# A causal convolution accumulated in the projection's PSUM bank, with buffer counts and stage order changed beside it

## The chip, the cores and the metric

The kernel runs on one core of a Trainium2 chip. The metric is the device time of one execution in microseconds. The engines are TensorE (PE, with its weight loads PEld), VectorE (DVE), ScalarE (ACT), GpSimd (POOL) and SyncE (SP, which here issues most DMAs). Each engine works through its own queue in order; semaphores tie the queues together.

## The reference

One layer of a decoder block over 2048 tokens of width 1024, in float32. Two mixers run side by side: four gated-DeltaNet heads and four retention heads, all of width 128. Then come the output projection, a gated MLP (5632 columns up, with a convolution of width 3) and a last norm. Cut to the part that matters here:

```python
n = _rms_norm(h, attn_norm_w[l])
proj = jnp.einsum('bsd,dc->bsc', n, w_in[l])
(gq, gk, gv, gg, ga, gb, rq, rk, rv, rg) = jnp.split(proj, split_idx, axis=-1)
# gated DeltaNet: short causal conv (4 taps) on q, k and v, then silu
qkv = jax.nn.silu(_causal_dwconv(jnp.concatenate([q, k, v], axis=-1), conv_w))
q = _l2norm(q) * (d ** -0.5); k = _l2norm(k)
# per chunk of 64: a triangular solve, and a recurrence over the chunks
t_mat = triangular_solve(eye + m, eye)
u = u_b - w_c @ state;  o = qd_c @ state + qk_c @ u
state = state * cd_c + kd_c.T @ u
# retention heads, concatenation, out projection, residual
h = h + jnp.einsum('bsm,md->bsd', mix, w_out[l])
n2 = _rms_norm(h, mlp_norm_w[l])
h = h + _conv_glu_mlp(n2, w_up[l], mlp_conv_w[l], w_down[l])
```

## The kernel before

A float32 product is made of three passes on TensorE: each operand is split into a high part and a rest, and `mm3` (lines 117 to 122) adds high x high, high x rest and rest x high in one PSUM bank. So nearly everything on PE comes in triples of rows, L120, L121 and L122, or L542 to L544 for the retention and gate projections.

The mixers work on four blocks b = 0 to 3 of 512 tokens. What is done for a block is cut into stages, and the string `ORDER` lists the stages of all blocks in the order in which the program is written out: "0a3" is stage a3 of block 0. The stages that matter here:

- aH: projection, convolution and Silu of k and q of DeltaNet head H (`proj_kq`); fH: the same for v (`proj_v`).
- cH: transposes of k and q (`kqtr`, L702), their norms, the products k kᵀ and k qᵀ (`kk`, L732), and the write of the matrix N to DRAM (`gdn_z`, L768). eH transposes v.
- bP: the inverse of 32x32 triangular blocks of head pair P on POOL (L784, L786), a round trip through DRAM (L789, L797) and a transpose on DVE (L799). lP: the two doubling levels, with `yps` (L814, L834) and `ttps` (L822, L841).
- rPc: step c of the recurrence of pair P: `ks` (L865), DVE L868, `wps` (L876), DVE L879, `sps` (L885), DVE L892 or L898.
- hH and yH: retention head H: `rtr` (L990), `rkk` (L996), the decay on DVE (L997), `ro` (L1011 and L1013), then L1016 on ACT and L1023 on DVE.
- dH the decay matrix, k, q, v the retention projections, p, P, g, G the gates, W and S the output projection as seven products of half matrices, O and Q the making of its weights (POOL L297, ACT L305, DVE L306), N the second norm, U a piece of the MLP's up projection.

`ORDER` sets the order of the program only. Below it a scheduler fixes the order of each engine's queue, and gives tiles their places: the numbers of buffers (`BUFS` for SBUF tiles, `NPB`, `NPM` and `NPR` for the three PSUM pools "bk", "mx" and "rc", which share the eight banks) are upper bounds that steer it. So a small edit may move instructions far from it.

A convolution of one head runs like this. PE makes the product `chm` in a bank of pool "bk": 24 matmuls of 128x512. DVE multiplies it by the row of inverse norms into the first half of an SBUF tile `ca` (L667, in `scaled`). ACT copies this, times the last tap, to the second half of `ca` (L414). DVE adds the other three taps there (L417), for b > 0 the three tokens of the block before (L421), and keeps the last three tokens for the next block (L423). ACT takes the Silu from the second half into the tile `ykq` (L680), or for v back into `ca` (L688). So the bank is free again after L667. A tile `ca` is two halves of 128x512, and the four heads of a block take twelve of them.

Of the kernel before, what the change touches and what calls it, by code (L numbers as in the profile page):

```python
# [10 lines left out]
AF = mybir.ActivationFunctionType  # L11
ALU = mybir.AluOpType
# [16 lines left out]
NWV = 5  # L29
FX = (0, 2, 4, 1, 5)  # L30
NU = 4
NPB = 9
NPM = 4
NPR = 10
NRAW = 3
NLATE = 4
NXR = 8
FD = 6
BUFS = {"n1": 8, "ykq": 3, "kv": 7, "NT": 7, "AT": 9, "o": 6, "n2s": 15, "xk": 2, "og": 1, "co": 6, "Cw": 3, 
        "wx": 1, "wsq": 5, "wvr": 1, "wvt": 8, "ca": 12, "mix": 5, "D": 6, "rk": 14, "rq": 4, "rv": 9,   # L40
        "sm": 6, "sc": 16, "wg": 2, "kt": 4, "Ar": 2, "Nb": 6, "rot": 1, "rrow": 6}

ORDER = ("0pro 0k0 0v0 0dec 0q0 0d0 0a0 0c0 0a1 0d1 0a2 0c1 0f1 0f0 0b0 0e0 0d2 0e1 0c2 0h0 0y0 0h1 0f2 "
# [11 lines left out]
P = 128  # L55
S = 2048
D = 1024
KT = D // P
TB = 512
NB = S // TB  # L60
NT = TB // P
# [10 lines left out]
U1 = 1024  # L72
# [147 lines left out]
def mixers(ctx, tc, base, base_used, marks, drp, mm3, gamma, mhalf, n1w, n2w, gcw, gv127, epsr, gnw, n2d, hd,  # L220
# [6 lines left out]
    PE, ACT, DVE, POOL = nc.tensor, nc.scalar, nc.vector, nc.gpsimd  # L227
# [4 lines left out]
    psm = ctx.enter_context(tc.tile_pool(name="psm", bufs=NPM, space=PSUM))  # L232
    psr = ctx.enter_context(tc.tile_pool(name="psr", bufs=NPR, space=PSUM))

# [40 lines left out]
    ghalo = pc(12, 3)  # L275
# [109 lines left out]
    def al(tag, shape, dt=F32):  # L385
        return unit(ap_, tag, shape, dt, **({"bufs": BUFS[tag]} if tag in BUFS else {}))

    def half(owner, key, tag, i):

        if key not in owner:  # L390
            owner[key] = al(tag, [P, 2, TB])
        return owner[key][:, i]
# [20 lines left out]
    def conv(ps, acc, wt, halo, first, ntap):  # L413
        ACT.activation(acc, ps, AF.Copy, scale=wt[:, ntap - 1:ntap])  # L414
        for s in range(1, ntap):
            w = wt[:, ntap - 1 - s:ntap - s]
            DVE.scalar_tensor_tensor(acc[:, s:], ps[:, :TB - s], w, acc[:, s:], op0=ALU.mult, op1=ALU.add)  # L417
        if not first:
            for s in range(1, ntap):
                w = wt[:, ntap - 1 - s:ntap - s]  # L420
                DVE.scalar_tensor_tensor(acc[:, :s], halo[:, ntap - 1 - s:], w, acc[:, :s],  # L421
                                         op0=ALU.mult, op1=ALU.add)
        DVE.tensor_copy(halo, ps[:, TB - (ntap - 1):])  # L423

    def A_items(b, st):
# [233 lines left out]
        def chmajor(w, i):  # L659
            n1 = st["n1"]  # L660
            ps = bank("chm")
            mm3(ps, [wcol(w, i, k) + (n1[k][:, 0], n1[k][:, 1]) for k in range(KT)])
            return ps

        def scaled(ps):
            ca = al("ca", [P, 2, TB])
            DVE.tensor_tensor(ca[:, 0], ps, st["rrow"], op=ALU.mult)  # L667
            return ca[:, 0], ca[:, 1]


        def proj_kq(h):
            def f(w):
                hd_ = st["hd", h] = {}
                ykq = hd_["ykq"] = al("ykq", (P, 2, TB))
                for i in range(2):
                    ps = chmajor(w, i)
                    ci = (4 if i == 0 else 0) + h
                    cin, acc = scaled(ps)
                    conv(cin, acc, gcw[:, ci], ghalo[:, ci], b == 0, 4)
                    ACT.activation(ykq[:, i], acc, AF.Silu)  # L680
            return f

        def proj_v(h):
            def f(w):
                ps = chmajor(w, 0)
                cin, acc = scaled(ps)
                conv(cin, acc, gcw[:, 8 + h], ghalo[:, 8 + h], b == 0, 4)
                ACT.activation(acc, acc, AF.Silu)  # L688
                st["hd", h]["v"] = acc
            return f  # L690

        def gdn_kq(h):
# [842 lines left out]
```

## Time and profile before

| | us |
|---|---|
| median of 3 runs (lowest to highest) | 2435.12 (2432.28 to 2436.66) |
| the profiled execution | 2431.43 |
| its span | 2429.6 |
| PE busy in it | 2382.8 (98%) |
| DVE busy | 1639.0 (67%) |
| ACT busy | 1052.5 (43%) |
| POOL busy | 448.7 (18%) |

The mixers fill about the first 1150 us of the span, the MLP's two projections the rest. A row of a group, as "L417 DVE ... x144 | 109.9, 763 | 20.0 <-ACT ca L414 19.0", has the line, engine, operation, output and inputs, the count, the busy time in us, the mean of one in ns, then the idle time of the engine just before them and what ended most of it. A row of a waits view has what waited for what, us in all, how often, and the longest. A row of a timeline has start and length in us, and in brackets the idle time before it and what ended it. A matmul of 128x512 is shown some 0.39 us long, but one starts every 0.227 us.

### The profile page before, as it was taken

Reading aid. Unit: us, or ns where it says so; the run is one execution under the profiler, and the core shown is the slowest. Engines: PE = TensorE matmul, PEld = TensorE weight load, DVE = VectorE, ACT = ScalarE, POOL = GpSimd, SP = SyncE. Lnnn points to the kernel's source line nnn. Section 1 sums busy time; section 2 is a strip of 40 time slices with the busy share of each in tenths; the row PEclk is TensorE's granted clock in tenths of the full one; section 3 lists DMA queues with packets and bytes.
Section 4 is the critical chain, followed back from the end, with each engine's and each line's share of the span. In section 5 each row is a group of like instructions: output and inputs, shape, how many; then the busy total and the mean of one; then the engine's idle time right before and its main releaser. Section 6 shows DMA issues by size and latency. Waiting matters only on the chain.

```text
span 2429.6 us, 35733 instructions
## 1 busy us (share of the span) xinstructions
PE 2382.8 (98%) x12364; PEld 1999.4 (82%) x12364; DVE 1639.0 (67%) x3137; ACT 1052.5 (43%) x2256; POOL 448.7 (18%) x745
## 2 busy tenths in 40 slices
PE   9998999999999999999999999999999999999998
PEld 8877888878887888887888888878888888888887
DVE  5866776664635673668988888995556676554773
ACT  6545555644444463356643434432222234332341
POOL 0166114520044003310101100100000002431020
PEclk9999999999999999999999999999999999999999
DMA  6877799895756865687977779877768588774782
GB/s 241 301 279 249 306 332 346 317 347 210 268 201 239 334 209 178 239 322 286 348 292 290 296 293 362 308 256 243 250 231 313 199 272 277 253 228 141 226 254 102
DMA packets 305414, 646.09 MB, mean 266 GB/s; under 512 B 50833, under 2 KB 130129, under 8 KB 305233
## 3 DMA queue, kind: packets, MB, share of 16 engines
q1 hardware_dynamic: 288512, 629.51, 72.7%
q10 hardware_dynamic: 16720, 14.30, 1.9%
q8 instruction: 97, 1.59, 0.3%
q14 instruction: 85, 0.69, 0.1%
HBM read 437.82 MB, written 205.88 MB: 265 GB/s over the span
## 4 chain that ended last, share of the span: by engine, by line
PE 51%; DVE 2%; issue 1%; ACT 0%; DMA 0%; POOLq 0%; POOL 0%; ACTq 0%
PE p L120 11%; PE p L121 11%; PE p L122 11%; PE d L122 6%; PE d L120 6%; PE d L121 6%; PE wo L122 0%; PE wo L120 0%; PE wo L121 0%; DVE x L1146 0%; DVE acc L1275 0%; DVE st L1167 0%; DVE uc L1228 0%; DMA wur<-in_w_u 0%; PE nps L1124 0%
## 5 line engine op out<-in xcount | busy, mean ns | idle before, releaser
L121 PE MATMUL p<-x,wu 128*128 128x512 f32 x1176 | 457.6, 389 | 0.0
L120 PE MATMUL p<-x,wu 128*128 128x512 f32 x1176 | 453.2, 390 | 1.1 <-ACT wu L1145 0.8
L122 PE MATMUL p<-x,wu 128*128 128x512 f32 x1176 | 451.1, 389 | 0.0
L120 PEld LDWEIGHTS p<-x,wu 128*128 128x128 f32 x1176 | 220.7, 188 | 49.1 <-DVE uc L1228 1.3
L121 PEld LDWEIGHTS p<-x,wu 128*128 128x128 f32 x1176 | 220.7, 188 | 45.9 <-DVE x L1146 0.5
L122 PEld LDWEIGHTS p<-x,wu 128*128 128x128 f32 x1176 | 220.7, 188 | 45.7
L1275 DVE SCALAR_TENSOR_TENSOR acc<-uc,base,acc 128x1022 f32<-128x1022 f32 (+1 forms) x176 | 220.7, 1278 | 38.0 <-ACT acc L1272 37.9
L1228 DVE TENSOR_TENSOR uc<-p,uc 128x512 f32<-128x512 f32 x224 | 153.0, 686 | 119.7 <-PE p L122 117.8
L542 PE MATMUL tok<-wc,n 128*128 128x512 f32 (+2 forms) x576 | 199.7, 353 | 7.2 <-ACT n L458 5.3
L543 PE MATMUL tok<-wc,n 128*128 128x512 f32 (+2 forms) x576 | 199.9, 349 | 0.0
L544 PE MATMUL tok<-wc,n 128*128 128x512 f32 (+2 forms) x576 | 195.4, 347 | 0.0
L191 POOL TENSOR_TENSOR vt<-vr 128x512 f32<-128x512 f32 x44 | 71.1, 1618 | 640.4 <-DMA vr<-in_w_d 464.0
L120 PE MATMUL d<-v,uu 128*128 128x512 f32 x448 | 174.3, 389 | 0.0
L121 PE MATMUL d<-v,uu 128*128 128x512 f32 x448 | 174.3, 389 | 0.0
L122 PE MATMUL d<-v,uu 128*128 128x512 f32 x448 | 174.3, 389 | 0.0
L120 PE MATMUL chm<-n,wc 128*128 128x512 f32 x384 | 152.2, 397 | 0.1
L122 PE MATMUL chm<-n,wc 128*128 128x512 f32 x384 | 151.2, 394 | 0.0
L121 PE MATMUL chm<-n,wc 128*128 128x512 f32 x384 | 151.0, 393 | 0.0
L1272 ACT ACTIVATE acc<-uc,base 128x1024 f32<-128x1024 f32 x88 | 97.1, 1144 | 80.7 <-DVE uc L1228 32.9
L542 PEld LDWEIGHTS tok<-wc,n 128*128 128x128 f32 x576 | 110.2, 192 | 20.2 <-ACT n L458 5.6
L417 DVE SCALAR_TENSOR_TENSOR ca<-ca,base 128x511 f32<-128x511 f32 (+1 forms) x144 | 109.9, 763 | 20.0 <-ACT ca L414 19.0
L543 PEld LDWEIGHTS tok<-wc,n 128*128 128x128 f32 x576 | 110.7, 192 | 12.5
(285 smaller groups left out, 5028.8 us busy)
## 6 DMA issues: line engine op xcount, KB each, us to landing
wu<-wu SPq DMA_DIRECT2D x308, 512.0 KB, 6.3
wc<-wd SPq DMA_DIRECT2D x116, 512.0 KB, 6.5
wv<-kW SPq DMA_DIRECT2D x112, 512.0 KB, 6.9
wc<-kP SPq DMA_DIRECT2D x84, 512.0 KB, 6.5
ur<-au SPq DMA_DIRECT2D x56, 512.0 KB, 5.7
wd<-wc SPq DMA_DIRECT2D x44, 512.0 KB, 4.7
wur<-in_w_u SPq DMA_DIRECT2D x44, 512.0 KB, 6.3
au<-st SPq DMA_DIRECT2D x88, 256.0 KB, 5.0
```

The lines of the kernel that those rows point to most:

```text
L120: PE.matmul(ps, ah, bh, start=(first and i == 0), stop=False, skip_group_check=chk)
L121: PE.matmul(ps, ah, bl, start=False, stop=False, skip_group_check=chk)
L122: PE.matmul(ps, al, bh, start=False, stop=(i == n - 1), skip_group_check=chk)
L191: POOL.tensor_tensor(tt[:, j], a, b_, op=ALU.subtract)
L417: DVE.scalar_tensor_tensor(acc[:, s:], ps[:, :TB - s], w, acc[:, s:], op0=ALU.mult, op1=ALU.add)
L542: PE.matmul(ps, ah, wh, start=(k == 0), stop=False)
L543: PE.matmul(ps, ah, wl, start=False, stop=False)
L544: PE.matmul(ps, al_, wh, start=False, stop=(k == KT - 1))
L1228: add = lambda o, ps, a: DVE.tensor_tensor(o, ps, a, op=ALU.add)
L1272: ACT.activation(acc, u, AF.Copy, scale=mcw[:, ci, 2:3])
L1275: DVE.scalar_tensor_tensor(acc[:, t:], u[:, :T2 - t], w, acc[:, t:], op0=ALU.mult, op1=ALU.add)
```

## The change

The change has three parts, and the diff has all of them.

First, `scaled` goes, and `conv_silu(ps, out, ci)` takes the place of three calls. The multiply by the row of inverse norms writes into the tile in which the result will stand: a half of `ykq` for k and q, a half of `ca` for v. The Copy with the last tap then writes into the product's own bank, the multiply-adds accumulate in that bank, and the Silu reads the bank and writes over the scaled input. `conv` itself is the same function with other arguments. For v, two heads share one `ca` tile, so that a block takes two of them.

Second, upper bounds of pools are changed: one more for "bk", one less for "rc", and fifteen counts of SBUF tiles.

Third, `ORDER` is another permutation of the stages. In the diff below its first line stands for it.

```diff
-NPB = 9
+NPB = 10
 NPM = 4
-NPR = 10
+NPR = 9
...
-BUFS = {"n1": 8, "ykq": 3, "kv": 7, "NT": 7, "AT": 9, "o": 6, "n2s": 15, "xk": 2, "og": 1, "co": 6, "Cw": 3, 
-        "wx": 1, "wsq": 5, "wvr": 1, "wvt": 8, "ca": 12, "mix": 5, "D": 6, "rk": 14, "rq": 4, "rv": 9, 
-        "sm": 6, "sc": 16, "wg": 2, "kt": 4, "Ar": 2, "Nb": 6, "rot": 1, "rrow": 6}
+BUFS = {"n1": 8, "ykq": 3, "kv": 9, "NT": 7, "AT": 9, "o": 8, "n2s": 17, "xk": 2, "og": 2, "co": 6, "Cw": 5, 
+        "wx": 1, "wsq": 5, "wvr": 1, "wvt": 7, "ca": 11, "mix": 3, "D": 7, "rk": 14, "rq": 4, "rv": 8, 
+        "sm": 6, "sc": 15, "wg": 2, "kt": 3, "Ar": 3, "Nb": 5, "rot": 2, "rrow": 6}
-ORDER = ("0pro 0k0 0v0 0dec 0q0 0d0 0a0 0c0 0a1 0d1 0a2 0c1 0f1 0f0 0b0 0e0 0d2 0e1 0c2 0h0 0y0 0h1 0f2 "
-         "0d3 0a3 0c3 0l0 0O0 0y1 0f3 0r00 0e2 0r01 0r02 0e3 0r03 0O2 0kq 0b1 0l1 0O1 0r10 0r11 0p0 1pro "
+ORDER = ("0pro 0k0 0dec 0v0 0q0 0a0 0d0 0c0 0a1 0d1 0a2 0c1 0d2 0f1 0f0 0e0 0b0 0e1 0c2 0h0 0y0 0f2 0h1 "
+         "0d3 0a3 0O0 0y1 0c3 0l0 0f3 0r00 0r01 0r02 0e2 0r03 0e3 0O2 0kq 0h2 0b1 0l1 0r10 0O1 0r11 0p0 "
...
-        def scaled(ps):
-            ca = al("ca", [P, 2, TB])
-            DVE.tensor_tensor(ca[:, 0], ps, st["rrow"], op=ALU.mult)
-            return ca[:, 0], ca[:, 1]
-
+        def conv_silu(ps, out, ci):
+            DVE.tensor_tensor(out, ps, st["rrow"], op=ALU.mult)
+            conv(out, ps, gcw[:, ci], ghalo[:, ci], b == 0, 4)
+            ACT.activation(out, ps, AF.Silu)
 
         def proj_kq(h):
             def f(w):
                 hd_ = st["hd", h] = {}
                 ykq = hd_["ykq"] = al("ykq", (P, 2, TB))
                 for i in range(2):
-                    ps = chmajor(w, i)
-                    ci = (4 if i == 0 else 0) + h
-                    cin, acc = scaled(ps)
-                    conv(cin, acc, gcw[:, ci], ghalo[:, ci], b == 0, 4)
-                    ACT.activation(ykq[:, i], acc, AF.Silu)
+                    conv_silu(chmajor(w, i), ykq[:, i], (4 if i == 0 else 0) + h)
             return f
 
         def proj_v(h):
             def f(w):
-                ps = chmajor(w, 0)
-                cin, acc = scaled(ps)
-                conv(cin, acc, gcw[:, 8 + h], ghalo[:, 8 + h], b == 0, 4)
-                ACT.activation(acc, acc, AF.Silu)
-                st["hd", h]["v"] = acc
+                v = st["hd", h]["v"] = half(st, ("cv", h // 2), "ca", h % 2)
+                conv_silu(chmajor(w, 0), v, 8 + h)
             return f
```

Every engine has as many instructions as before. From line 691 on a line of the changed kernel has a number 8 smaller than before (L865 becomes L857, L1023 becomes L1015); L667 becomes L666, and both Silus become L668.

The first place is the convolution of k and q of head 3 in block 0 (stage a3) on DVE. `chm` are the products' banks, `wc` and `wg` pieces of weights that DVE makes beside it. The queue before:

```order
L667 TENSOR_TENSOR ca_1448<-chm_1423,rrow_247 128x512
L365 TENSOR_TENSOR wc_1496<-wraw_1490,wc_1496 128x512
L423 COPY pers1_117<-ca_1448 128x3
L417 SCALAR_TENSOR_TENSOR ca_1448<-ca_1448,base_60 128x511
L417 SCALAR_TENSOR_TENSOR ca_1448<-ca_1448,base_60 128x510
L417 SCALAR_TENSOR_TENSOR ca_1448<-ca_1448,base_60 128x509
L365 TENSOR_TENSOR wc_1501<-wraw_1502,wc_1501 128x512
L306 TENSOR_TENSOR wg_1695<-wvr_1656,wg_1695 128x512
L667 TENSOR_TENSOR ca_1481<-chm_1456,rrow_247 128x512
```

And of the change, from the row of the retention head that stands ahead of it:

```order
L1015 SCALAR_TENSOR_TENSOR pers4_405<-pers4_405,pers5_1294 128x4
L215 TENSOR_TENSOR wc_1745<-wraw_1740,wc_1745 128x512
L215 TENSOR_TENSOR wc_1750<-wraw_1748,wc_1750 128x512
L666 TENSOR_TENSOR ykq_1415<-chm_1416,rrow_247 128x512
L666 TENSOR_TENSOR ykq_1415<-chm_1448,rrow_247 128x512
L423 COPY pers1_117<-ykq_1415 128x3
L306 TENSOR_TENSOR wg_1907<-wvt_1884,wg_1907 128x512
L423 COPY pers1_117<-ykq_1415 128x3
L417 SCALAR_TENSOR_TENSOR chm_1416<-ykq_1415,base_60,chm_1416 128x511
L417 SCALAR_TENSOR_TENSOR chm_1448<-ykq_1415,base_60,chm_1448 128x511
L417 SCALAR_TENSOR_TENSOR chm_1416<-ykq_1415,base_60,chm_1416 128x510
```

Before, all of this stood far ahead of the retention head's L1023; now it stands behind it, with the two products' instructions interleaved.

The second place is on PE, in block 3, where the levels of pair 1 (`yps`, `ttps`) run between recurrence steps. Before:

```order
L885 MATMUL sps<-pers_1301,AT 128x128 x2
L865 MATMUL ks<-pers_124,ykq 128x128 x4
L834 MATMUL yps<-NT 64x64 x8
L841 MATMUL ttps<-AT,pers_117 64x64 x4
L583 MATMUL mxt<-base,mix 128x128 x4
L841 MATMUL ttps<-AT,pers_117 64x64 x4
L583 MATMUL mxt<-base,mix 128x128 x4
L876 MATMUL wps<-kv,AT 128x128 x2
```

Of the change (`wo` is the output projection):

```order
L122 MATMUL wo<-wv,wu_11536 128x512
L826 MATMUL yps<-NT 64x64 x8
L877 MATMUL sps<-pers_1294,AT 128x128 x2
L857 MATMUL ks<-pers_124,ykq 128x128 x4
L833 MATMUL ttps<-AT,pers_117 64x64 x4
L982 MATMUL rtr<-base,rk 128x128 x4
L982 MATMUL rtr<-base,rq 128x128 x4
L833 MATMUL ttps<-AT,pers_117 64x64 x4
```

The sps and ks that stood ahead of yps now stand between yps and the first ttps.

The third place is on PE in block 1, a retention head beside the levels (`P` is a gate's product). Before:

```order
L841 MATMUL ttps<-AT,pers_117 64x64 x4
L996 MATMUL rkk<-ykq 128x128 x4
L1011 MATMUL ro<-rv,Ar 128x128
L1013 MATMUL ro<-pers_124,ykq 128x128
L1011 MATMUL ro<-rv,Ar 128x128
```

Of the change:

```order
L833 MATMUL ttps<-AT,pers_117 64x64 x4
L988 MATMUL rkk<-ykq 128x128 x4
L868 MATMUL wps<-kv,AT 128x128 x2
L120 MATMUL P<-wc,sc 128x512
L121 MATMUL P<-wc,sc 128x512
L122 MATMUL P<-wc,sc 128x512
L120 MATMUL P<-wc,sc 128x512
L121 MATMUL P<-wc,sc 128x512
L122 MATMUL P<-wc,sc 128x512
L877 MATMUL sps<-pers_1294,kv 128x128 x2
L877 MATMUL sps<-pers_1294,AT 128x128 x2
L1003 MATMUL ro<-rv,Ar 128x128
```

Between rkk and ro, which needs what DVE makes of rkk, there are now two wps, six products of 128x512 and four sps.

20 rows, old and new, of the table ORDER are left out of this document.

## The prediction

> **What bounds the kernel now.** I read the head of the page first, then the busy time by stretches, then PE's waits.
>
> ```profile
> span 2429.6 us, 35733 instructions
> PE 2382.8 (98%) x12364; PEld 1999.4 (82%) x12364; DVE 1639.0 (67%) x3137; ACT 1052.5 (43%) x2256; POOL 448.7 (18%) x745
> ...
> 0.00:50.00 50.00, 44.65 (x267) 40.60 (x268) 26.52 (x72) 31.58 (x67) 3.18 (x13) 1.00 0.66 242
> 50.00:1150.00 1100.00, 1065.93 (x6482) 908.29 (x6481) 704.76 (x1799) 558.09 (x1504) 302.39 (x613) 0.99 0.76 275
> 1150.00:2400.00 1250.00, 1249.28 (x5518) 1031.86 (x5517) 898.35 (x1250) 458.84 (x677) 140.94 (x115) 1.00 0.76 264
> ```
>
> The lower rows give stretch, length, busy time of PE, PEld, DVE, ACT and POOL, PE's granted clock, DMA share, GB/s. PE is the bound: it is idle for 2429.6 - 2382.8 = 46.8 us. Of these 1100 - 1065.9 = 34.1 us lie in the mixers (50 to 1150 us), where the change works, and 0.7 us in the MLP. DVE is 64% busy there (704.8 of 1100) and ACT 51%: work added to or taken from them matters only where PE waits for its result. PE has the same matmuls before and after, so the change can win or lose only in PE's waits and in the clock:
>
> ```profile
> 1095.57:1098.98 3.41, 3.41 (x19) 2.89 (x19) 3.38 (x11) 1.42 (x4) 1.60 (x2) 0.50 1.04 417
> sum 23.87, PE 23.75 PEld 19.89 DVE 15.02 ACT 13.08 POOL 4.38; mean PE 3.39 PEld 2.84 DVE 2.15 ACT 1.87 POOL 0.63
> ```
>
> The first row is one stretch at clock 0.50, the second the sum over all seven such stretches; half of 23.87, about 12 us, is what they cost. The waits, in all, times, longest:
>
> ```profile
> PE wps L876 <- DVE kv L868: 4.7, 2, 2.7
> PE sps L885 <- DVE pers L879: 2.9, 5, 0.8
> PE kqtr L702 <- ACT ykq L680: 2.6, 1, 2.6
> PE yps L814 <- DVE NT L799: 2.5, 1, 2.5
> PE ttps L841 <- DVE pers L837: 2.3, 1, 2.3
> PE yps L834 <- DVE NT L827: 2.1, 2, 1.5
> PE ro L1011 <- DVE Ar L997: 0.8, 1, 0.8
> PE ttps L822 <- DVE pers L818: 0.6, 1, 0.6
> ```
>
> They are many and small. No row names the convolution's own arithmetic except the third: transposes of q and k that wait for a Silu.
>
> **The convolution's operations.** Removed is nothing: per product there are still one multiply, one Copy with the last tap, three multiply-adds, for blocks 1 to 3 three halo adds, one halo copy and one Silu. What changes is where they read and write.
>
> ```profile
> L417 DVE SCALAR_TENSOR_TENSOR ca<-ca,base 128x511 f32<-128x511 f32 (+1 forms) x144 | 109.9, 763 | 20.0 <-ACT ca L414 19.0
> L667 DVE TENSOR_TENSOR ca<-chm,rrow 128x512 f32<-128x512 f32 x48 | 32.8, 686 | 25.4 <-PE chm L122 20.2 <-PE wo L122 2.3 <-PE mxt L583 2.1
> L1146 DVE TENSOR_TENSOR wu<-st,wu 128x512 fp32r<-128x512 f32 x88 | 56.9, 685 | 0.5 <-ACT wu L1145 0.5
> L215 DVE TENSOR_TENSOR wc<-wraw,wc 128x512 fp32r<-128x512 f32 x16 | 11.6, 725 | 11.9 <-ACT wc L214 11.9
> L680 ACT ACTIVATE ykq<-ca 128x512 f32<-128x512 f32 x32 | 20.0, 630 | 28.2 <-DVE ca L421 15.9 <-DVE ca L417 9.6 <-PE chm L122 2.6
> L1248 ACT ACTIVATE uc<-p 128x512 f32<-128x512 f32 x42 | 24.8, 591 | 161.3 <-PE p L122 161.2
> ```
>
> The Silu will read a bank: the row that does (L1248) has 591 ns against 630, so 48 x 39 ns = 1.9 us less for ACT. A multiply from a bank costs DVE 686 ns, from SBUF 685: reading is free. Writing to a bank by DVE or ACT stands nowhere in this trace. I bound the multiply-add by the fastest and slowest pieces of that size among these rows, 685 and 763 + 77 (the mean and as much again above it): 144 x (-78 to +77 ns) = -11 to +11 us of DVE work, and take 0, since the reading side shows no difference. DVE has 395 us free in the mixers, so neither end reaches PE directly; in one convolution it is +-0.24 us on a chain.
>
> The Trainium skill ("Perfetto Trace Analysis", section "Optimizing Scalar/DVE Operations") gives DVE an access overhead of about 60 ns per instruction on SBUF and 125 on PSUM, and ScalarE 93 and 51. By it the 144 + 108 accumulations would cost DVE an estimated 252 x 65 ns = 16 us more and ACT 96 x 42 ns = 4 us less. The 686 against 685 ns above doesn't show it for reading; for writing no row here can say. By it the sum would be the same, 16 us being 4% of DVE's free time.
>
> **Place 1, block 0, head 3 (a3, c3).** Before, the convolution worked in `ca` tiles and only the Silu needed `ykq`. Now the first multiply writes `ykq`, and both multiplies stand behind the retention head's L1015 in DVE's queue (the rows of the order above). But a3 is also further ahead of its reader: between the same neighbours PE has 12.7 us more work before the transposes (the matmuls that moved ahead, by their durations in this trace).
>
> ```profile
> 146.14 1.28 POOL L297 TENSOR_TENSOR wvt<-wvr,wvt 128x512 f32<-128x512 f32 x1
> ...
> 147.45 0.63 ACT L305 ACTIVATE wg<-wvt 128x512 fp32r<-128x512 f32 x1 [6.56 <-POOL wvt L297]
> ...
> 148.99 1.14 ACT L680 ACTIVATE ykq<-ca 128x512 f32<-128x512 f32 x2
> ...
> 149.66 1.64 PE L702 MATMUL kqtr<-base,ykq 128*128 128x128 f32 x8 [2.55 <-ACT ykq L680]
> 151.09 3.12 PE L732 MATMUL kk<-ykq 128*128 128x256 f32 x8
> ...
> 151.75 0.16 DVE L1023 SCALAR_TENSOR_TENSOR pers<-pers,pers 128x4 f32<-128x4 f32 x1 [0.61 <-ACT pers L1019]
> 155.16 1.02 POOL L1024 TENSOR_TENSOR pers<-pers,base 128x4 f32<-128x4 f32 x1
> ```
>
> Before, the wait came from POOL: ACT stood 6.56 us at L305 for a difference that POOL made inside its triangular base, and the Silus behind it came late. After, PE arrives at 149.66 - 2.55 + 12.7 = 159.8. By DVE alone the k Silu is ready after L1015 (151.9), three L215 (2.18), two multiplies (1.37), two halo copies and one wg piece (1.04, as their kinds last elsewhere), five multiply-adds (3.8) and the Silu (0.6): 160.9, a wait of 1.1. By ACT: POOL's differences now stand four steps (8 rows) later in the base; the 19 rows from 147.42 to 155.16 take 0.41 each, so ACT gets past L305 at 150.7, reaches the L214 that DVE's L215 needs at 154.7, and the same DVE rows end at 163.0: a wait of 3.2. I take the middle, 2.15, against 2.55: **-0.4**. Ends: -2.55 (no wait), and +6.6 (POOL late once more by that row's 6.56).
>
> **The next link, yps of pair 1, block 0.** Behind the kk products come z1, POOL's base, a DRAM round trip and yps.
>
> ```profile
> 167.73 0.79 ACTq L768 DMA_DIRECT2D z<-NT  x2
> 179.65 0.24 POOL L784 TENSOR_TENSOR pers<-Nb,pers 128x31 f32<-128x31 f32 x1 [4.25 <-DMA Nb<-z]
> 183.74 1.29 POOL L297 TENSOR_TENSOR wvt<-wvr,wvt 128x512 f32<-128x512 f32 x1
> 219.57 0.54 POOL L786 TENSOR_TENSOR pers<-pers 128x8 f32<-128x8 f32 x1
> 233.45 0.45 PE L814 MATMUL yps<-NT 128*32 128x32 f32 x16 [2.54 <-DVE NT L799]
> ```
>
> The last kk comes 12.7 + 6.8 = 19.5 us of PE work later, so z1 starts at about 178 to 180, some 10.5 to 12.5 after 167.73. POOL's stretch of 40.2 us held seven L297 of 1.29; now five stand in it: 37.6. Adding 11.9 from z1 to the base and 13.3 from the base's end to yps gives 241 to 243; PE arrives 8.8 us of work later than 230.9, at 239.3 to 240.4. The wait stays about what it was: **0**, ends -2.5 and +2.6 (the 40.2 kept).
>
> **Block 1 and block 3 pieces.** In block 1 `ro` stood right behind `rkk` (0.8 us wait); now two wps, six 512-wide matmuls and four sps, about 2.7 us, stand between, and yps L834 gets a like cover for 0.7 of its 2.1: **-1.5**, ends 0 and -2.3. In block 3, pair 1, the transposes ttps waited 2.3 us right behind yps; now two sps and four ks stand between, whose groups last 0.55 and 0.99 here, so 1.5 are covered; thirteen wo matmuls (13 x 0.227 = 2.95) cover the 0.6 of L822; and if the gap goes, so does the half-clock stretch behind it at 1095.57 (1.6): **-3.7**, ends 0 and -4.
>
> **Tighter recurrence.** The links ks, wps, sps with under 1 us of PE work between are 13 before and 18 after, of 92. The row has 2.9/5 = 0.6 us for such a wait, so 5 more cost up to 3; I take **+1.5**, ends 0 and +5.
>
> **Banks.** The product's bank is now held until the Silu has ended; before, until the multiply. Measured over the 48 products, that hold is 5 to 32 us, mostly 6 to 10; the next user of the bank stands some 15 us of PE work behind in the new order. All are covered but block 1's first five (and two in block 2, by 0.7 us).
>
> ```profile
> 259.99 0.39 PE L122 MATMUL chm<-n,wc 128*128 128x512 f32 x1
> ...
> 271.66 0.68 DVE L667 TENSOR_TENSOR ca<-chm,rrow 128x512 f32<-128x512 f32 x1
> ...
> 291.08 1.15 ACT L680 ACTIVATE ykq<-ca 128x512 f32<-128x512 f32 x2
> 294.79 0.39 PE L122 MATMUL chm<-n,wc 128*128 128x512 f32 x1
> ...
> 303.88 0.68 DVE L667 TENSOR_TENSOR ca<-chm,rrow 128x512 f32<-128x512 f32 x1
> 310.14 0.63 ACT L688 ACTIVATE ca<-ca 128x512 f32<-128x512 f32 x1 [4.17 <-DVE ca L421]
> ```
>
> The first of them ended near 260, its Silu at about 291.7, 32 us against 26.9 of PE work: 5.1 short. The fifth: 310.8 - 295.2 = 15.6 against 6.6, 9.0 short. The ones between fall into the shadow of these two. So 0 to 14.1; since the hold is long only because DVE and ACT came 9 to 20 us late there, in an order that is gone, I take **+1.0**.
>
> **Sum:** -0.4 + 0 - 1.5 - 3.7 + 1.5 + 1.0 = -3.1 us. Against the profiled execution (2431.4 in all, 1.8 around its span) 2428.3; against the median of the runs shown, 2435.1, it is **2432**. This kernel tells about 0.2%, 4.9 us, from no change, so the forecast is no change, leaning faster.
>
> **Rivals.**
> R1, slower: the bank becomes the wait. PE stands at the first write into a bank whose convolution isn't through. Price: both shortfalls and a half-clock stretch of 1.7 behind each, 14.1 + 3.4 for the +1.0: -3.1 + 16.5 = +13.4, 2448.5; with the fifth product alone +6.6, 2441.7; between them 2445. It decides when a hold exceeds the PE work to the bank's next writer, so about 27 us for the first and 6.6 for the fifth. For it speak the ACT and DVE delays of these rows, against it the 15 us elsewhere. A rule agrees with it: the Trainium skill ("PSUM — Partial Sum Buffer", "Summary: rules for kernel authors") says to evacuate promptly since the memory is tight. Before, every evacuation here was the multiply alone; no run yet shows the other.
> R2, slower: a3 comes late behind the freed `ykq` and POOL (+6.6 in place of -0.4) and yps with it (+2.6): -3.1 + 7.0 + 2.6 = +6.5, 2442.
> R3, faster by more: two `ca` tiles per block instead of twelve, and the larger pools, let loads and copies start early, so that waits shrink throughout. The worst 50-us windows lose
>
> ```profile
> sum 350.00, PE 322.21 PEld 273.51 DVE 238.86 ACT 187.38 POOL 112.49; mean PE 46.03 PEld 39.07 DVE 34.12 ACT 26.77 POOL 16.07
> ```
>
> 27.8 us in these seven windows; half of it and half of the clock's 12 is -19.9, with the +2.5 of banks and links -17.4: 2418. For it: the many small waits, all in the mixers; against: they name short chains, not loads.
> R4: nothing moves, the waits go from one row to another of the same length: 2435.
>
> **How the numbers follow.** Forecast 0.42, its own range 2427 to 2437, of which 0.12 lies below 2430.2 and 0.30 within; R3 0.26; R4 0.06; R1 0.18; R2 0.08. Faster 0.12 + 0.26 = 0.38, same 0.36, slower 0.26. The range goes from 2415, beyond R3's middle, to 2447, between R1's middle and its full price.
>
> **What would show it.** Right: PE's idle in 50 to 1150 us near 31; kqtr waiting 1 to 3 us for L668; yps L806 still waiting about 2.5; ttps L833 under 1; no wait of PE's 512-wide writes for ACT's L668 as the freer of a bank. R1: PE rows of mxt or tok that wait for ACT L668 for 3 us or more near 260 to 300. R2: kqtr waiting over 6 us. R3: PE idle below 20. L417 outside 0.69 to 0.84 us would break the bound on the writes. The forecast is wrong if the mixers' idle falls or rises by more than 5 us.

## The result and the profile after

The changed kernel takes 2410.74 us (median of 4 runs, 2409.45 to 2415.96), against 2433.78 for the kernel before: a ratio of 0.9908, with a 95% interval of 0.9889 to 0.9927. It is some 22 us faster. The forecast was no change, 2432, in a range of 2415 to 2447: the measured time lies below the range, and the gain is clear of the noise. The rival R3 (2418) came nearest by time.

The page and the busy time by stretches of the changed kernel, and last the sum over the stretches at half clock:

```profile
span 2407.7 us, 35677 instructions
PE 2370.7 (98%) x12364; PEld 1995.4 (83%) x12364; DVE 1652.5 (69%) x3137; ACT 1052.7 (44%) x2256; POOL 422.9 (18%) x745
...
50.00:1130.00 1080.00, 1055.21 (x6478) 903.30 (x6477) 715.00 (x1796) 556.85 (x1502) 277.12 (x613) 1.00 0.77 278
1130.00:2378.00 1248.00, 1247.97 (x5520) 1032.84 (x5519) 901.48 (x1253) 459.98 (x677) 140.40 (x115) 1.00 0.77 265
...
sum 10.24, PE 9.91 PEld 8.84 DVE 8.78 ACT 9.50 POOL 0.00; mean PE 3.30 PEld 2.95 DVE 2.92 ACT 3.17 POOL 0.00
```

The span is 21.9 us shorter, and nearly all of that lies in the mixers: by the measure of lost time that the experiments use, some 2 us lie behind them. PE's idle time fell from 46.8 to 2407.7 - 2370.7 = 37.0: that is 9.8. In the mixers alone it fell from 34.1 to 1080 - 1055.2 = 24.8, by 9.3, past the 5 us at which the prediction called itself wrong, and not to the under 20 that R3 asked for. The half-clock stretches fell from 23.87 to 10.24 us, half of which is lost time: 6.8. The other 5.3 are in PE's busy time, in rows that last longer than their kind, mostly near a wait; I can't split them further, since the ends of matmuls are modelled. The waits of PE, in all, times, longest:

```profile
PE tok L542 <- ACT n L458: 5.4, 1, 5.4
PE mxt L583 <- DVE mix L581: 3.7, 1, 3.7
PE tok L542 <- ACT o L864: 3.3, 1, 3.3
PE sps L877 <- DVE pers L871: 3.0, 4, 1.3
PE ttps L833 <- DVE pers L829: 1.8, 2, 1.0
...
PE wps L868 <- DVE kv L860: 1.1, 2, 0.5
PE ks L857 <- DVE pers L882: 1.0, 1, 1.0
...
PE ro L1003 <- DVE Ar L989: 1.0, 1, 1.0
...
PE yps L806 <- DVE NT L791: 0.2, 1, 0.2
```

The first row is the start of the kernel and was there before. Gone, or nearly, are the waits of kqtr (2.6), of yps (2.5 and 2.1, now 0.5 by this row and a smaller one) and of wps (4.7, now 1.1). Two are new: mxt with 3.7 and tok with 3.3 us. No row has PE waiting for a Silu to free a bank.

The convolution's groups of the changed kernel, in the same columns as before:

```profile
L417 DVE SCALAR_TENSOR_TENSOR chm<-ykq,base,chm 128x511 f32<-128x511 f32 (+2 forms) x96 | 71.2, 749 | 11.1 <-ACT chm L414 9.7
L417 DVE SCALAR_TENSOR_TENSOR chm<-ca,base,chm 128x511 f32<-128x511 f32 (+2 forms) x48 | 35.9, 748 | 5.2 <-ACT chm L414 4.6
...
L414 ACT ACTIVATE chm<-ykq,base 128x512 f32<-128x512 f32 x32 | 22.0, 692 | 48.8 <-DVE ykq L666 48.7
L668 ACT ACTIVATE ykq<-chm 128x512 f32<-128x512 f32 x32 | 18.8, 593 | 23.9 <-DVE pers L423 16.9 <-DVE chm L417 6.9
```

An accumulation in the bank takes 749 ns, in SBUF it took 763; the Silu went from 630 to 593 ns, and the Copy from 722 to 692, by this row of the kernel before:

```profile
L414 ACT ACTIVATE ca<-ca,base 128x512 f32<-128x512 f32 x48 | 34.5, 722 | 76.1 <-DVE ca L667 72.5 <-issue 3.3
```

### The profile page after: what moved, and what is told of

Its sections match the earlier page's. It is cut to its first block, busy times and chain, and to the rows that moved or that the text cites. A ratio compares the mean times of both kernels' runs of the same rounds, so it can differ in the third digit from the quotient of the medians.

```text
span 2407.7 us, 35677 instructions
## 1 busy us (share of the span) xinstructions
PE 2370.7 (98%) x12364; PEld 1995.4 (83%) x12364; DVE 1652.5 (69%) x3137; ACT 1052.7 (44%) x2256; POOL 422.9 (18%) x745
## 4 chain that ended last, share of the span: by engine, by line
PE 85%; DMA 6%; DVE 4%; ACT 2%; issue 2%; POOL 1%; SPq 0%; ACTq 0%; POOLq 0%; DVEq 0%
PE p L120 11%; PE p L121 11%; PE p L122 11%; PE d L120 6%; PE d L121 6%; PE d L122 6%; PE tok L542 3%; PE tok L544 3%; PE tok L543 3%; PE chm L120 3%; PE chm L122 3%; PE chm L121 3%; PE wo L120 2%; PE wo L122 2%; PE wo L121 2%
## 5 line engine op out<-in xcount | busy, mean ns | idle before, releaser
L542 PEld LDWEIGHTS tok<-wc,n 128*128 128x128 f32 x576 | 109.8, 192 | 22.1 <-ACT n L458 5.4
L543 PEld LDWEIGHTS tok<-wc,n 128*128 128x128 f32 x576 | 110.2, 191 | 13.1 <-DVE wc L215 0.7
L544 PEld LDWEIGHTS tok<-wc,n 128*128 128x128 f32 x576 | 108.2, 191 | 12.2
```

Source lines behind the costliest of these rows:

```text
L542: PE.matmul(ps, ah, wh, start=(k == 0), stop=False)
L543: PE.matmul(ps, ah, wl, start=False, stop=False)
L544: PE.matmul(ps, al_, wh, start=False, stop=(k == KT - 1))
```

## The experiments

All ratios are to the kernel before, run on the same chip beside it, with 95% intervals. A measure that several readings use was worked out from the traces. For each pair of PE's matmuls in a row it takes the time from start to start, less the median of that for the same shape, and sums what is over zero by how much PE work had been done (the time since the first matmul, less what had been lost by then). So the columns line up between kernels, and a column is what PE lost in that piece of the program (us). The columns have hard edges: with PE's work counted by the medians alone, 200 to 250 has 20.2 for e_conv and 11.7 for the change, where the table has 23.1 and 8.1. So a difference of 3 us in a single column says little:

```
PE work done (us)    100-150  150-200  200-250  250-300  400-500  650-750  950-1050   all
before                  9.2     10.1     10.6      6.5     15.6     15.0      15.3   110.5
change                  3.1     10.2      8.1      9.7     11.5      8.8      10.3    87.6
e_conv                  1.9      8.4     23.1      6.0     19.2     13.3      17.7   121.0
e_conv_caps             1.9      8.1     23.1      8.3     13.1     11.8      18.9   115.4
e_conv_order            7.0     10.6      6.2     10.7     13.4     21.5      13.9   114.6
e_order_caps            7.7     12.0      9.9      4.9     15.4     14.6      16.4   116.6
h_before_to57           1.9      9.8     18.9     10.7     11.7      8.8      10.6   104.0
h_after_to57            2.4     11.0      6.5     17.7     10.7     15.6      19.9   115.1
e_v_own                 2.1      5.4     15.5      5.6     15.0      8.8      11.8    96.9
x_conv_ca               6.8     12.7     10.0      9.8     13.5     17.1      17.9   112.9
```

### The three parts, alone and in pairs

The change has three parts: the convolution (`scaled` to `conv_silu`, v in halves of a tile), the buffer counts, and the stage order. Each run takes the kernel before and puts in some of them:

```diff
e_conv:        + conv_silu
e_order:                     + ORDER
e_caps:                               + NPB, NPR, BUFS
e_order_caps:                + ORDER  + NPB, NPR, BUFS
e_conv_order:  + conv_silu   + ORDER
e_conv_caps:   + conv_silu            + NPB, NPR, BUFS
```

> The convolution in the bank alone, with the stage order and the buffer counts of before. Theory A (the stage order makes the gain, by putting PE work between dependent steps): no change, ratio to before 0.998 to 1.003, and the PE waits of before (wps, kqtr, yps, each some 2.5 us and a half-clock stretch) are still there. Theory B (the convolution makes it, by a shorter chain and by SBUF that comes free): ratio 0.990 to 0.994. Theory C (the order was fitted to the convolution, and each part alone gives nothing): 0.999 or above.

> The new stage order alone, with the old convolution and the old buffer counts. A: ratio 0.990 to 0.995, fewer half-clock stretches than the seven of before. B: 0.998 to 1.002. C: 1.000 or above, with waits in new places.

> The new buffer counts alone. A and B: within 0.2% of before (0.998 to 1.002). C: 1.000 or above.

> Stage order and buffer counts of the change, with the old convolution (each v head takes a ca tile again, twelve per block where eleven is the bound). A: ratio 0.990 to 0.993, all of the gain. B: 0.998 to 1.002. C: 0.997 or above.

> Convolution in the bank and the new order, with the old buffer counts. Theory C1 (order and convolution are the pair that matters; counts only trim): ratio 0.990 to 0.995. C2 (all three are fitted to one queue order, and any one undone loses the gain): 0.999 or above.

> Convolution in the bank and the new buffer counts, with the old order. C1: 1.000 to 1.004, like the convolution alone (1.0036). C2: 0.999 or above as well. If the counts are what makes the convolution pay (B'), 0.990 to 0.995.

| kernel | median us | ratio | interval |
|---|---|---|---|
| convolution alone | 2440.71 | 1.0036 | 1.0021 to 1.0050 |
| order alone | 2445.14 | 1.0056 | 1.0041 to 1.0071 |
| counts alone | 2438.81 | 1.0027 | 1.0017 to 1.0038 |
| order and counts | 2437.98 | 1.0031 | 1.0019 to 1.0042 |
| convolution and order | 2435.89 | 1.0017 | 1.0008 to 1.0027 |
| convolution and counts | 2438.75 | 1.0036 | 1.0023 to 1.0049 |
| all three (the change) | 2410.74 | 0.9908 | 0.9889 to 0.9927 |

Theories A, B and C1 fall; C and C2 hold. None of the six is faster than before, and all three together are 22 us faster. So no part has a gain of its own that could be added up. What the table of lost time shows is where each undone part costs. The convolution with the old order loses 23 us between 200 and 250, where the change loses 8. With the old counts the change loses 21.5 between 650 and 750, where it loses 8.8. With the old convolution (e_order_caps) no one place carries the loss: six of the seven columns are 2 to 6 us above the change's.

### Places

If the order counts place by place, a kernel with the change's order up to some stage and the old one from there should carry each one's losses in its own piece.

```diff
h_before_to57:
-ORDER = (the change's 271 stages)
+ORDER = (stages 1 to 57 as before, "0pro" to "0y3"; then the change's)
h_after_to57:
-ORDER = (the change's 271 stages)
+ORDER = (stages 1 to 57 as in the change; then as before)
n_after_early:
-ORDER = ("0pro 0k0 0dec 0v0 0q0
+ORDER = ("0pro 0k0 0v0 0dec 0q0
```

> The changed kernel with the first 57 stages (block 0, up to the second retention output) in the order of before, the other 214 in the order of the change. Theory D: what decides is, place by place, whether a late GpSimd or ScalarE result stands ahead of the recurrence in VectorE's queue; the convolution alone lost 12 us between 200 and 250 us that way (one gap of 5.3 us and two half-clock stretches behind a normalisation on GpSimd). D says that gap is back and the later gains stay: 0.995 to 0.999. If the order of block 0 doesn't matter: 0.990 to 0.993.

> The mirror: the first 57 stages in the order of the change, the others in the order of before; convolution and buffer counts of the change. D, place by place: the 8 us gained before 250 us stay, the 15 us gained later are lost: 0.995 to 0.999. If the parts are independent of each other, this and its mirror share the difference between the change (0.991) and the same with all of the old order (1.0036).

> The changed kernel with one pair of neighbouring stages at the very start swapped back (0dec behind 0v0); PE's queue keeps its order, VectorE's and ScalarE's change in places. If the gain sits in PE's order: 0.990 to 0.993. If it is a fit of all queues to each other that any shift breaks: 0.994 or above.

The first gave 0.9964 (0.9953 to 0.9975), its mirror 1.0034 (1.0021 to 1.0047). In the table the first has the old loss at 200 to 250 (18.9) and from 400 on nearly the change's own numbers (11.7, 8.8, 10.6). The mirror has about the change's number at 200 to 250 (6.5) and losses like the old order's later on (15.6 and 19.9, where e_conv_caps has 11.8 and 18.9), though not at 400 to 500 (10.7). So most of the losses sit in places and follow the stage order of that place. The mirror's total missed its range, since a new loss came at the seam (17.7 at 250 to 300) and the later ones were larger than what I had taken from the kernel before. The third stayed at 0.9924 (0.9907 to 0.9941), the same as the change within the intervals. It shows less than was expected of it: in its trace the rows of PE, VectorE, GpSimd and SyncE all stand in the change's order, as far as names without buffer numbers tell, and on ScalarE only two DMA issues (L760) moved by a few rows. So it is nearly the change once more; what a real shift of the other queues would do with PE's order kept was not run.

### Freed tiles, the final tile, the bank

Three variants of the changed kernel take the convolution apart:

```diff
e_v_own:
-                v = st["hd", h]["v"] = half(st, ("cv", h // 2), "ca", h % 2)
+                v = st["hd", h]["v"] = al("ca", [P, 2, TB])[:, 0]
e_psum_ca:
-            DVE.tensor_tensor(out, ps, st["rrow"], op=ALU.mult)
-            conv(out, ps, gcw[:, ci], ghalo[:, ci], b == 0, 4)
+            cin = al("ca", [P, 2, TB])[:, 0]
+            DVE.tensor_tensor(cin, ps, st["rrow"], op=ALU.mult)
+            conv(cin, ps, gcw[:, ci], ghalo[:, ci], b == 0, 4)
e_sbuf_sum:
-            conv(out, ps, gcw[:, ci], ghalo[:, ci], b == 0, 4)
-            ACT.activation(out, ps, AF.Silu)
+            acc = al("ca", [P, 2, TB])[:, 1]
+            conv(out, acc, gcw[:, ci], ghalo[:, ci], b == 0, 4)
+            ACT.activation(out, acc, AF.Silu)
```

> The changed kernel, but each v head has a ca tile of its own again, as before, instead of two heads in one. If SBUF that comes free is the mechanism (my rival R3): 0.996 or above. If not: 0.990 to 0.993.

> The changed kernel, but the scaled input goes into a ca tile of its own instead of the final tile; sum and Silu from the bank stay. If the wait for a free final tile (my rival R2) costs anything, this is faster than the change by 2 to 7 us; if the sum in the bank is what helps, it is the same as the change (ratio to before 0.990 to 0.993); if the freed SBUF is what helps, it loses most of it (0.997 or above).

> The changed kernel, but the sum is kept in an SBUF tile ca; the scaled input goes straight into the final tile. If holding the bank costs (my rival R1), this is as fast as the change or faster by up to 10 us; if freed SBUF or the fitted order is what helps, 0.997 or above. The Copy and the multiply-adds should go back from 0.69 and 0.75 us to 0.72 and 0.76.

They gave 0.9934 (0.9918 to 0.9951), 0.9963 (0.9950 to 0.9976) and 1.0059 (1.0042 to 1.0076). The v tiles are worth 6 us of 22 at most: against n_after_early, which ran beside it on the same chip, it is 2 by the ratios, and the intervals overlap. Taking the final tile out of the first multiply doesn't help here but costs 13 us; putting the sum back into SBUF costs 37. In that run the operations did go back (Copy 724, Silu 630, multiply-adds 774 ns for k and q). None of the three is a clean price of its edit: of PE's 12364 rows 1480, 1921 and 2387 have another row in their place than in the change, and by the runs above a new order alone can cost this much. So freed SBUF, R3's mechanism, is small for the v tiles and open for those of k and q: both runs that give every product a tile of its own again lose most or all of the gain, but with another order. Freed tiles alone, in the convolution alone, bring nothing. As for R1 and R2, neither edit freed any time, and the changed kernel's waits name neither.

### What made the convolution alone slow

The largest loss of the convolution alone is at 200 to 250. Its timeline has a chain through five queues (SP's and ACT's rows, then POOL's, DVE's and PE's):

```profile
218.90 0.33 SPq L369 DMA_DIRECT2D wd<-wc  x1
228.74 2.52 SPq L781 DMA_DIRECT2D z<-pers  x4
231.31 1.07 SPq L225 DMA_DIRECT2D xk<-in_x  x2
...
235.35 1.06 ACT L431 ACTIVATE xk<-xk 128x1024 f32<-128x1024 f32 x1 [8.04 <-DMA xk<-in_x]
...
232.74 0.40 POOL L773 COPY pers<-base 128x256 f32<-128x256 f32 x1 [4.03 <-DMA z<-pers]
233.10 1.02 POOL L905 TENSOR_TENSOR pers<-pers,base 128x4 f32<-128x4 f32 x1
...
234.15 1.14 DVE L581 SCALAR_TENSOR_TENSOR mix<-o,pers,mix 128x128 f32<-128x128 f32 x4 [6.12 <-POOL pers L905]
235.20 0.60 DVE L860 SCALAR_TENSOR_TENSOR kv<-ks,pers,kv 128x128 f32<-128x128 f32 x2
...
235.60 1.22 PE L868 MATMUL wps<-kv,AT 128*128 128x128 f32 x4 [5.30 <-DVE kv L860]
```

POOL's base of pair 1 ends at 228.7. SP's queue stands for its result from 219.2; the loads of x behind it come late, and ACT stands 8.0 us for them. POOL's normalisation L905 stands behind a copy (L773) that waits 4.0 us for the DMAs that carry the base's result away, DVE's L581 stands for L905, the recurrence's L860 stands behind L581, and PE stands 5.3 us. Three links were taken out, one at a time:

```diff
x_conv_recip (on e_conv, in gdn_fin):
-                POOL.tensor_tensor(fr, so, mhalf[:, :4], op=ALU.pow)
+                DVE.reciprocal(fr, so)
x_conv_zq, b_zq, x_before_zq (on e_conv, on the change, on the kernel before):
                 for g in range(4):
-                    nc.sync.dma_start(z2.rearrange(
+                    POOL.dma_start(z2.rearrange(
x_conv_ca (on e_conv): as e_psum_ca above
```

> The convolution alone (stage order and counts of before), and the normalisation of the recurrence's output (GpSimd's power, L905) replaced by a reciprocal on VectorE: the square root is left out. In the convolution alone PE stood 5.3 us at 230 us: L905 stood on GpSimd behind a copy that waited for a DMA, VectorE's L581 stood for L905, and L860 of the recurrence stood behind L581. Theory D (that queue position is the price, not the convolution): the gap and its two half-clock stretches go, and the time is 5 to 12 us below the convolution alone: ratio to before 0.998 to 1.002. If the gap has another cause, 1.003 or above and a gap of over 3 us stays near 230.

> The convolution alone, with the four DMAs that write the result of GpSimd's base to DRAM (L781) issued on GpSimd's queue instead of SyncE's. In the convolution alone SyncE's queue stood from 219.2 to 228.7 us for the base, the loads of x behind it came late, ScalarE stood 8.0 us for them, and with it VectorE and the recurrence. Theory E (SyncE's queue behind the base is the price of the old order): the gap of over 4 us near 230 goes, with its half-clock stretches, ratio to before 0.994 to 1.000. If not E: 1.003 or above, with the gap there.

> The same edit on the changed kernel, where SyncE stands 5.7 us for that base. E: the gap of 3.4 us at 219 us shrinks and the time is up to 6 us below the change (ratio to before 0.988 to 0.991), if the queues' new order costs nothing elsewhere. A refitted order that loses elsewhere: 0.993 or above.

> The same edit on the kernel before. E: a small gain, 0.995 to 0.999, since the waits behind the base there are one of 2.2 and one of 2.5 us with one half-clock stretch. Otherwise 1.000 or above.

> The convolution alone, with the scaled input in a ca tile of its own, so that only the Silu needs the final tile; sum in the bank, old order, old counts. Theory F: the price of the old order is that the first multiply waits for a free final tile, by which head 3's projection, its transposes and GpSimd's base of pair 1 come some 8 us later (base 192 to 228 us there, 180 to 219 before), and all that stands behind the base with them. F: base near 179 to 218, the loss between 200 and 250 us gone (23 back to 11 us or less), ratio to before 0.996 to 1.000. If not F: 1.002 or above, with the loss still there.

The reciprocal gave 1.0052 (1.0035 to 1.0068). DVE's and PE's rows of that run:

```profile
228.30 0.60 DVE L860 SCALAR_TENSOR_TENSOR kv<-ks,pers,kv 128x128 f32<-128x128 f32 x2
238.55 1.20 DVE L306 TENSOR_TENSOR wg<-wvr,wg 128x512 fp32r<-128x512 f32 x1 [9.65 <-ACT wg L305]
239.68 0.41 DVE L871 TENSOR_TENSOR pers<-wps,pers 128x256 f32<-128x256 f32 x1
...
240.14 1.05 PE L877 MATMUL sps<-pers,kv 128*128 128x128 f32 x4 [4.66 <-DVE pers L871]
```

L860 came 7 us earlier, as theory D said, and PE lost as much all the same: now L871, the next link, stood behind an L306 that waited for ACT, and ACT for its late load. So D's link was real but not the root.

With the base's DMAs on POOL's queue it got worse, 1.0115 (1.0100 to 1.0130): POOL now stood 4.1 us in issuing them, and L905 with the rest behind it:

```profile
232.94 0.58 POOL L781 DMA_DIRECT2D z<-pers  x1 [4.12 <-issue]
235.97 1.03 POOL L905 TENSOR_TENSOR pers<-pers,base 128x4 f32<-128x4 f32 x1
...
237.04 2.14 DVE L581 SCALAR_TENSOR_TENSOR mix<-o,pers,mix 128x128 f32<-128x128 f32 x4 [7.42 <-POOL pers L905]
...
240.17 1.22 PE L877 MATMUL sps<-pers,kv 128*128 128x128 f32 x4 [7.38 <-DVE pers L871]
```

On the changed kernel the same edit gave 0.9993 (0.9984 to 1.0003), on the kernel before 1.0049 (1.0032 to 1.0066): it costs 12 to 21 us everywhere. So E's forecast failed in all three. That SyncE's stand costs nothing isn't shown by it: the loads of x did go out 5 us earlier (226.3 instead of 231.3), but POOL now stood instead, and in the changed kernel the gap at 219 us shrank from 3.3 to 2.6 us while one of 7.3 came up at 497 us.

What the runs with this loss share is a late base. Over all 20 kernels, the base of pair 1 in block 0 ends at 226.6 to 228.7 us in the five that lose 18.9 to 25.5 us at 200 to 250 of the table (the convolution alone, with the counts, h_before_to57, x_conv_recip and x_conv_zq). It ends at 216.7 to 225.5 in the other fifteen, which lose 5.0 to 15.5. That the base is the cause isn't shown by this: the five share one convolution and one order of block 0, and among the fifteen a later base doesn't go with a larger loss (220.2 us with 15.5, 221.8 with 8.1). The last run asked whether it is late because the first multiply waits for a free final tile. The busy times of 200 to 250 us of the convolution alone and of x_conv_ca, in this order:

```profile
200.00:250.00 50.00, 39.67 (x264) 34.99 (x265) 28.13 (x64) 25.16 (x57) 31.94 (x56) 0.90 0.77 266
```

```profile
200.00:250.00 50.00, 44.27 (x324) 37.95 (x322) 29.77 (x55) 26.50 (x62) 27.32 (x49) 0.97 0.81 276
```

The loss at that place is gone (10.0 instead of 23.1 in the table, PE idle 5.7 instead of 10.3 us), but the base came only 4.7 us earlier (224.0 instead of 228.7), not 8, and the whole kernel was at 1.0013 (1.0003 to 1.0022), between F's two ranges: 4.9 us came back at 100 to 150 and some 4 at 650 to 750. So theory F named the place and an edit that removes the loss; its size for the base was wrong, and since this edit too gives PE a new order, that the final tile alone does it is not shown. The changed kernel speaks against it: there the two multiplies into the final tile start at 149.5 us, as late as in the convolution alone (148.8), and yet the base ends at 221.8 and that loss doesn't come.

### A try at a faster kernel

```diff
b_late_gate (on the change):
-... 1a0 0g1 0G1 1dec 1f0 1q0 1a3 ...
+... 1a0 0g1 1dec 1f0 1q0 0G1 1a3 ...
```

> A try at the largest gap that the change still has (3.7 us at 311 us, transposes of the gated output that wait for VectorE's L581, itself behind GpSimd's L1016): the change with stage 0G1 two stages later, behind 1f0 and 1q0, so that fewer of these transposes stand together. If PE then finds other work: 2 to 7 us faster than the change (ratio to before 0.988 to 0.990). If the first transpose waits just as long: no difference, 0.990 to 0.993; any loss elsewhere, above.

It gave 0.9956 (0.9941 to 0.9971): slower than the change. Its gap at the transposes stayed, and a second wait of tok, of 5.0 us, came up at 435 us. Its waits:

```profile
PE tok L542 <- ACT o L864: 8.7, 2, 5.0
PE P L120 <- DMA wc<-kP: 5.4, 4, 1.8
...
PE mxt L583 <- DVE mix L581: 3.9, 1, 3.9
```

None of the variants was faster than the change.

## Why the prediction was wrong, point by point

**The bound** was read rightly: PE's work is the same, and nearly all of the gain is in the mixers, in waits and clock.

**The convolution's operations** were rightly taken as free. The accumulation lies inside the bound that I gave (0.69 to 0.84 us), at 0.749. Nothing of the 16 us that the Trainium skill's overheads ("Perfetto Trace Analysis", section "Optimizing Scalar/DVE Operations") would give DVE shows in that row, nor in the halo additions (L421: 222 ns before and after). The Copy and the Silu became faster by 30 and 37 ns, in the direction of that page's figures for ScalarE in the Trainium skill, 93 ns on SBUF and 51 on PSUM.

**Place 1** had the right chain and the wrong times. The rows of the changed kernel:

```profile
155.62 0.58 ACT L668 ACTIVATE ykq<-chm 128x512 f32<-128x512 f32 x1
158.72 0.58 ACT L668 ACTIVATE ykq<-chm 128x512 f32<-128x512 f32 x1
...
160.49 0.60 PE L694 MATMUL kqtr<-base,ykq 128*128 128x128 f32 x4
...
177.90 0.31 ACTq L760 DMA_DIRECT2D z<-NT  x1
...
186.78 0.24 POOL L776 TENSOR_TENSOR pers<-Nb,pers 128x31 f32<-128x31 f32 x1 [9.40 <-DMA Nb<-z]
221.63 0.22 POOL L778 TENSOR_TENSOR pers<-pers 128x8 f32<-128x8 f32 x1
234.79 0.45 PE L806 MATMUL yps<-NT 128*32 128x32 f32 x16 [0.33 <-DVE pers L903]
```

PE came to kqtr at 160.5 (159.8 predicted), but the first Silu was done at 156.2, not at 160.9 to 163.0, so there was no wait at all: -2.6 and a half-clock stretch, where the term said -0.4. The retention head's rows ahead of it in DVE's queue had come 6 us sooner than the 151.9 that I carried over from before (145.99 for L1015 in the changed kernel).

**The next link**: z1 went out at 177.9 (178 to 180 predicted). The base took 35.1 us instead of 37.6 and began at 186.8 instead of 190. PE too came there 5 us earlier than predicted, at 234.5 and not at 239 to 240. So yps waited 0.5 us in two rows, not the 2.5 of before: -2.0 and another half-clock stretch, where the term said 0.

**Block 1 and block 3 pieces**: about as predicted. The waits of yps L826 are gone, and that of ro in block 1 too (the 1.0 that ro has now is in block 0, at 141 us); in block 3 the waits of ttps are gone, and so is the stretch at half clock at 1095. In the table 950 to 1050 gained 5.0, against 3.7 in the term, though sps and rkk wait there now.

**Tighter recurrence** had the wrong sign. I priced the number of links without cover, +1.5. Waits of the kernel before that the prediction did not show:

```profile
PE P L120 <- ACT n2s L1125: 2.5, 1, 2.5
...
PE tok L542 <- ACT o L1016: 1.8, 1, 1.8
...
PE ks L865 <- DVE pers L892: 1.3, 3, 0.7
...
PE ks L865 <- DVE pers L890: 1.1, 1, 1.1
...
PE wps L876 <- ACT mix L556: 0.6, 1, 0.6
```

With 4.7 and 2.9 of the rows shown there, wps, sps and ks waited 4.7 + 0.6 + 2.9 + 1.3 + 1.1 = 10.6 us. After, the three rows in the section on the result have 1.1 + 3.0 + 1.0, and two smaller ones of sps 0.8: 5.9. The large ones before, wps at 221 and 496 us with over 2 us each, came from a VectorE that was late for another reason: rows ahead of its L868 stood for ScalarE.

```profile
218.06 0.69 DVE L306 TENSOR_TENSOR wg<-wvt,wg 128x512 fp32r<-128x512 f32 x1 [2.87 <-ACT wg L305]
...
496.84 0.16 DVE L911 SCALAR_TENSOR_TENSOR pers<-pers,pers 128x4 f32<-128x4 f32 x1 [2.57 <-ACT pers L901]
```

The count of links without cover doesn't see such waits.

**Banks**: +1.0 was an overestimate, no wait of that kind shows. R1 fell: a product's bank is now held until its Silu, and no wait of PE names that Silu.

**The step that failed** is the size of the sum's own terms, the recurrence's first. The table takes PE's waits by kind, from the rows shown and smaller ones of the same kinds, and adds 1.7 us for each half-clock stretch of before that followed one of them (at 150, 235, 498 and 1095 us) and is gone:

| term | forecast, us | waits before | waits after | stretches gone | comes to |
|---|---|---|---|---|---|
| place 1: kqtr | -0.4 | 2.6 | 0 | 1 | -4.3 |
| next link: yps of pair 1 | 0 | 2.5 | 0.5 | 1 | -3.7 |
| block 1 and 3: ttps, yps, ro | -1.5 - 3.7 | 5.8 | 2.8 | 1 | -4.7 |
| recurrence: ks, wps, sps | +1.5 | 10.6 | 5.9 | 1 | -6.4 |
| banks | +1.0 | 0 | 0 | 0 | 0 |
| together | -3.1 | 21.5 | 9.2 | 4 | -19.1 |

So the sum looked at the right kinds of wait and got their sizes wrong: 16 us lie between -3.1 and -19.1. Place 1 and the next link took the times of VectorE and GpSimd from the kernel before, and both came earlier. The recurrence was priced by a count of links, where the runs show that its two largest waits had another cause. And a wait was priced at its own length: the clock stood in the first part, with 12 us, but only block 3 carried a stretch of it, where four went. The waits outside the sum, which it let stand, didn't bring the gain: those for n2s (2.5 us) and of one tok (1.8) are gone, but mxt with 3.7 and another tok with 3.3 came, and in all they grew from about 11 to about 15 us, with three stretches before and three after. That leaves about 15.6 us gained in waits and clock, near the 9.8 + 6.8 of the profile; the rest is in waits under 0.2 us.

**The rivals.** R3 had nearly the time (2418 by half of the idle and half of the clock; measured -9.3 of 34.1 and -6.8 of 11.9). That is luck as far as the runs go: its mechanism, freed tiles, has at most 6 us for the v tiles by e_v_own, and what the other tiles and the larger pools are worth in this order isn't shown. R4 and R2 fell with the result. That one part alone could cost time, and that only the three together gain, was in none of them.

Still open: why the scheduler's order for exactly this combination is better than for the six others. The runs show that the losses follow the stage order, place by place, and that the largest single one goes with a late base on POOL and with what stands behind it on SP, ACT and DVE. They don't separate PE's order from that of the other queues. Nor do they show a rule by which one could have told the good order from a poor one beforehand.

## What to carry to other kernels

Where a scheduler fixes the queues, an edit's own cost may be nothing, and its effect through the order 20 us, as here; a part taken out of such a change measures the new order, not the part, so that parts alone and in pairs have to be run before any of them is credited. When a wait on a saturated engine is priced, add the half-clock stretch: here one followed every gap of 3 us or more and two thirds of those of 2 to 3. And cutting one link of a chain through in-order queues only helps if what stands at the next link is not late for the same reason.

## What the runs showed of the hardware

A gap on PE costs more than itself. Over the traces of 20 kernels in this study, counted from 30 us to the end of the mixers, all 43 PE gaps of 3 us or more were followed, within 8 us of their begin, by a stretch of at least 3.41 us at clock 0.50. Of 56 gaps of 2 to 3 us 37 were; of 76 gaps of 1.3 to 2 us 20, some of them beside a larger gap. Two stretches of 3.41 us at 316 us in the changed kernel followed one gap:

```profile
315.60 1.90 PE L583 MATMUL mxt<-base,mix 128*128 128x128 f32 x10 [3.70 <-DVE mix L581]
...
316.11:319.52 3.41, 3.08 (x15) 2.78 (x13) 2.99 (x10) 3.35 (x8) 0.00 (x0) 0.50 0.71 283
319.52:322.94 3.42, 3.42 (x10) 2.65 (x9) 3.27 (x12) 2.74 (x6) 0.00 (x0) 0.50 0.02 5
```

So that gap of 3.7 us cost about 3.7 + 3.4. The Trainium skill ("TensorE: Matmul & The Clock Gate", Part 1, on the clock gate) has windows of about 3.4 us that run free of the program, and the traces agree with the length; by the Trainium skill's rules there an idle window, or a gap of more than about 3.4 us, lowers the clock, and here gaps of two thirds of a window often did.

The second thing was the accumulation in PSUM: VectorE's multiply-add reading and writing a bank took 749 ns against 763 in SBUF, which is no difference beyond that between SBUF rows (e_sbuf_sum has 774 and 747), and ScalarE's Copy into a bank took 692 ns and its Silu out of one 593, against 722 and 630.
